# A gated mLSTM/S5 block: two operands transposed by VectorE alone, without the path through DRAM

## The chip, the cores and the metric

The kernel runs on one core of a Trainium2 chip. The metric is the device time of one execution in microseconds. Before the change the median of three runs is 1259.12 us (1258.21 to 1259.77).

## The reference, cut to what matters

One layer on a sequence of 256 rows with 2048 columns. The mLSTM and the S5 branch end in two projections to 2048 columns, which are gated and added (`merged`), projected by `w_out` and added to the residual; a SwiGLU feed-forward part with 5632 hidden columns follows.

```python
y_m = mlstm_branch(...) @ w_up_m          # 1024 -> 2048
y_s = s5_branch(...) @ w_up_s             # 512 -> 2048
g = sigmoid(p[..., c2:].reshape(b, s, 2, D) + b_gate)
merged = g[..., 0, :] * y_m + g[..., 1, :] * y_s
x = x + merged @ w_out                    # 2048 -> 2048
h2 = rms_norm(x, norm_ffn_g)
x = x + (silu(h2 @ w_ffn_gate) * (h2 @ w_ffn_up)) @ w_ffn_down
return rms_norm(x, norm_final_g)
```

## The kernel before

All weights come as blocks of 128 partitions x 1024 float32 columns (512 KB, two K tiles of 512 output columns), 432 of them in the order of use: `w_in`, the head matrices, `w_glu`, `w_up_s`, `w_up_m` (16 blocks), `w_out` (32), gate and up (176), down (88). A block is loaded by SyncE's queue (`emit_dma`, L144) into `raw`, which has three buffers; `emit_split` (L147) makes two reduced-precision parts of it, `hi` by a cast on ScalarE (L156) and `lo` = raw - hi on VectorE (recorded at L94, the line of the helper `TT`). Both have three buffers. `o2_block` (L160) then issues 12 matmuls for the block: two K tiles, two halves `tt` of 128 rows, and three products (activation hi x weight hi, hi x lo, lo x hi), at L100, into two accumulators of 128x512. A group of blocks with the same output columns is a chunk `n`: four blocks in `w_up_m`, eight in `w_out` and in the feed-forward matrices.

The activation is the stationary operand of a matmul, so it has to lie with its columns on the partitions. After a chunk of `w_up_m` the two tiles `merged` (rows x 512 columns, held in `gm`) have to be transposed to `mTh`/`mTl`, after a chunk of `w_out` the two tiles of the residual `x1` to `h2h`/`h2l`, and after each pair of gate and up chunks the hidden activation to `aT`.

`blocks_T` (L273) does that inside groups of 32 partitions: one VectorE instruction transposes all 32x32 blocks of a 128x512 tile in place of their group. The blocks must then change groups, and that goes through DRAM: `groups_dma` (L278) writes the tile out (`bounce`, L281) and reads four strided pieces back (L283), all on GpSimd's queue. `turn` (L969) is this path for `merged` and the hidden activation, `x1_T` (L1008) for the residual; a cast on ScalarE (L979, L1027) and a subtraction on VectorE then make the hi and lo parts. The steps are put off by `later`, which runs a step one or more weight blocks after it was handed in:

```python
def later(fn, delay=1):
    laters.append([delay, fn])
```

The program is built with a scheduler that orders the instructions of each engine by its own timeline. Within an engine they then run in that order, so a split of a weight block waits for whatever the scheduler put ahead of it on VectorE or ScalarE.

Of the kernel before, what the change touches and what calls it, by code (L numbers as in the profile page):

```python
# [13 lines left out]
AF = mybir.ActivationFunctionType  # L14
ALU = mybir.AluOpType
ADD, SUB, MUL, MAX, MIN = ALU.add, ALU.subtract, ALU.mult, ALU.max, ALU.min

P = 128
# [29 lines left out]
def block_kernel(ctx: ExitStack, tc: tile.TileContext, d, out):  # L48
    nc = tc.nc
    V, A, PE = nc.vector, nc.scalar, nc.tensor  # L50
# [12 lines left out]
    def nm(s):  # L63
        uid[0] += 1
        return f"{s}_{uid[0]}"

    def u8(shape, dt=F32, name="u"):
        return up.tile(shape, dt, tag="u8", name=nm(name), bufs=NU8)
# [10 lines left out]
    def m2(shape=(P, 512), dt=F32, name="m"):  # L79
        return tp.tile(list(shape), dt, tag="m2k", name=nm(name), bufs=NM2)  # L80

    def acc_tile():
        return pp.tile([P, 512], F32, tag="acc", name=nm("acc"), bufs=4)
# [4 lines left out]
    def TS(o, i, s1, s2=None, op0=MUL, op1=None):  # L88
        if op1 is None:
            return V.tensor_scalar(o, i, s1, None, op0=op0)  # L90
        return V.tensor_scalar(o, i, s1, s2, op0=op0, op1=op1)

    def TT(o, a, b, op):
        return V.tensor_tensor(o, a, b, op=op)  # L94

    def STT(o, a, s, b, op0, op1, **kw):
        return V.scalar_tensor_tensor(out=o, in0=a, scalar=s, in1=b, op0=op0, op1=op1, **kw)  # L97
# [4 lines left out]
    def f(ap):  # L102
        return ap.bitcast(F32)
# [5 lines left out]
    def pvs(n, i=None, w=1):  # L109
        a, b = PV[n]  # L110
        if i is None:
            return pv[:, a:b]
        return pv[:, a + i : a + i + w]
# [46 lines left out]
    def o2_block(acc, lhs, kts, hi, lo, first, last):  # L160
        n = len(kts)
        for q, kt in enumerate(kts):
            h = hi[:, q * 512 : (q + 1) * 512]
            l = lo[:, q * 512 : (q + 1) * 512]
            for tt in range(2):
                xh, xl = lhs(kt, tt)
                mm(acc[tt], xh, h, first and q == 0, False)
                mm(acc[tt], xh, l, False, False)
                mm(acc[tt], xl, h, False, last and q == n - 1)

    def lhs_of(hts, lts, per):
        def g(kt, tt):
            a, b = divmod(kt, per)
            s = slice(tt * 128, (tt + 1) * 128)
            return hts[a][:, b, s], lts[a][:, b, s]
        return g
# [64 lines left out]
    def rstd(o, ms, tag):  # L241
        w = ms.shape[-1]
        rc = cp.tile([P, w], F32, name=nm("rc"))
        V.reciprocal(rc, ms)
        A.activation(o, rc, AF.Sqrt)
        STT(rc, o, -0.5, ms, MUL, MUL)
        TT(rc, rc, o, MUL)
        STT(o, rc, 1.5, o, ADD, MUL)
# [24 lines left out]
    def blocks_T(o, i):  # L273
        V.transpose(o.rearrange("p j a c -> p a j c"), i.rearrange("p (a j c) -> p a j c", a=4, j=4))  # L274
# [3 lines left out]
    def groups_dma(dt_, st_):  # L278
        w = st_.shape[2]
        bounce = dp_.tile([P, 4, w], F32, tag=f"d{w}", name=nm("bounce"))  # L280
        nc.gpsimd.dma_start(bounce, st_)  # L281
        for j in range(4):
            nc.gpsimd.dma_start(  # L283
                dt_[32 * j : 32 * j + 32], bounce.rearrange("(i r) j x -> r i j x", i=4)[:, :, j]
            )
# [510 lines left out]
    cur = {}  # L796
# [47 lines left out]
    def gate_ap(key, tt, n):  # L844
        return cur[key][:, tt, n * 512 : n * 512 + 512]
# [105 lines left out]
    def upm_mm(i, nk, hi, lo):  # L951
        n, kp = nk
        if n == 0 and kp == 0:
            mlg.until("out")
            cur["mTh"] = [u8([P, 8, 256], F32R, name="mTh") for _ in range(2)]
            cur["mTl"] = [u8([P, 8, 256], F32R, name="mTl") for _ in range(2)]
        oh, ol = ml["out"]
        if kp == 0:
            cur["acc"] = [acc_tile(), acc_tile()]
        o2_block(cur["acc"], lhs_of([oh], [ol], 8), (2 * kp, 2 * kp + 1), hi, lo, kp == 0, kp == 3)  # L960
        if kp == 3:
            for tt in range(2):
                o = gate_ap("gm", tt, n)
                TT(o, cur["acc"][tt], o, MUL)
                TT(o, o, gate_ap("gs", tt, n), ADD)
                v = lambda a: a[n // 2][:, n % 2 * 4 : n % 2 * 4 + 4, :]
                turn(n, tt, o, v(cur["mTh"]), v(cur["mTl"]))

    def turn(n, tt, src, th, tl):  # L969
        st_ = m2([P, 4, 4, 32])  # L970
        blocks_T(st_, src)

        def move():
            dt_ = m2([P, 4, 4, 32])
            groups_dma(dt_.rearrange("p i a c -> p i (a c)"), st_.rearrange("p j a c -> p j (a c)"))

            def split():
                v = lambda a: a[:, :, tt * 128 : tt * 128 + 128].rearrange("p a (i c) -> p i a c", i=4)
                A.copy(v(th), dt_)  # L979
                TT(v(tl), dt_, f(v(th)), SUB)  # L980

            later(split)

        later(move)
# [3 lines left out]
    def out_mm(i, nk, hi, lo):  # L988
        n, kp = nk
        if n == 0 and kp == 0:  # L990
            cur["x1"] = u16([P, 2, 2048], name="x1")
            cur["h2h"] = [u8([P, 8, 256], F32R, name="h2h") for _ in range(2)]
            cur["h2l"] = [u8([P, 8, 256], F32R, name="h2l") for _ in range(2)]
        if kp == 0:
            cur["acc"] = [acc_tile(), acc_tile()]
            cs = slice(n * 512, n * 512 + 512)
            with tc.issue_after(wdma[0]):
                nc.sync.dma_start(cur["x1"][:, :, cs], d["x"].rearrange("(a p) c -> p a c", p=P)[:, :, cs])
        o2_block(cur["acc"], lhs_of(cur["mTh"], cur["mTl"], 8), (2 * kp, 2 * kp + 1), hi, lo, kp == 0, kp == 7)
        if kp == 7:  # L1000
            for tt in range(2):
                o = cur["x1"][:, tt, n * 512 : n * 512 + 512]
                TT(o, cur["acc"][tt], o, ADD)
                jk = t2()
                A.activation(jk, o, AF.Square, accum_out=ss2[:, tt, n : n + 1])
            later(lambda: x1_T(n))

    def x1_T(n):  # L1008
        sd = u8([P, 2, 1024], name="x1sd")
        st_ = sd[:, 0].rearrange("p (t j a c) -> p t j a c", j=4, t=2, a=4)  # L1010
        for tt in range(2):
            blocks_T(st_[:, tt], cur["x1"][:, tt, n * 512 : n * 512 + 512])

        def move():
            for tt in range(2):
                groups_dma(
                    sd[:, 1].rearrange("p (t i x) -> p t i x", t=2, i=4)[:, tt],
                    sd[:, 0].rearrange("p (t j x) -> p t j x", j=4, t=2)[:, tt],
                )
            later(split)  # L1020

        def split():
            d_ = sd[:, 1].rearrange("p (t i a c) -> p a (t i) c", i=4, t=2, a=4)
            for a in range(4):
                ct = 4 * n + a
                v = lambda h: h[ct // 8][:, ct % 8, :].rearrange("p (i c) -> p i c", c=32)
                A.activation(v(cur["h2h"]), d_[:, a], AF.Copy, scale=pvs("g2", ct))  # L1027
                STT(v(cur["h2l"]), d_[:, a], pvs("g2", ct), f(v(cur["h2h"])), MUL, SUB)

        later(move, 0)  # L1030
        if n == 3:
            s = cp.tile([P, 2], F32, name="ssum2")
            V.tensor_reduce(s, ss2, mybir.AxisListType.X, ADD)
            TS(s, s, 1.0 / D, EPS, MUL, ADD)
            rstd(r2, s, "r2")
# [117 lines left out]
    for b in range(2):  # L1153
        blocks.insert(len(blocks) - GLU, (d["w_glu"][0, b], glu_mm, (0, b)))
    add_mat("w_up_s", 4, 2, ups_mm)
    add_mat("w_up_m", 4, 4, upm_mm)
    add_mat("w_out", 4, 8, out_mm)
    fg, fu = ffn_mm("fg"), ffn_mm("fu")
# [10 lines left out]
    def later(fn, delay=1):  # L1169
        laters.append([delay, fn])  # L1170
# [63 lines left out]
    for i in range(len(blocks)):  # L1234
# [30 lines left out]
        for l in run:  # L1265
            l[1]()
        fn, (n, kp) = blocks[i][1], blocks[i][2]
        t = 2.59 if fn in (win_mm, ups_mm, upm_mm) else 1.31
        if fn is win_mm and kp == 7 and n > 4:
            t -= 1.3  # L1270
        if i < 6:
            t = 1.14 + SLACK + EB
# [82 lines left out]
```

## Time and profile before

| | |
|---|---|
| median of three runs | 1259.12 us |
| profiled execution | 1258.85 us, span 1257.1 us |
| TensorE busy | 1233.7 us (98%), 5738 matmuls |
| VectorE busy | 803.8 us (64%) |
| ScalarE busy | 604.0 us (48%) |
| GpSimd busy | 106.6 us (8%) |
| queue q1 (SyncE's loads) | 237.25 MB, 58.1% of 16 DMA engines |
| queue q0 (GpSimd's transfers) | 19.94 MB, 4.8% |

PE is TensorE, PEld its weight load, DVE is VectorE, ACT is ScalarE, POOL is GpSimd, SP is SyncE; a q behind the name is the engine's sequencer. The profile comes from one execution; a busy time is the sum over instructions without their overlap. TensorE's busy share says little by itself: its matmuls are pipelined, and a matmul lasts about 0.39 us while the next starts 0.23 us after it. Where a row merges several instructions (x2), its length runs from the start of the first to the end of the last.

### The profile page before, as it was taken

How to read it: one execution, taken by the hardware profiler on the slowest of the kernel's cores; microseconds unless marked ns; L12 is line 12 of the kernel's file. 1: busy time of each engine (PE TensorE's matmuls, PEld its weight loads, DVE VectorE, ACT ScalarE, POOL GpSimd, SP SyncE). 2: the span in 40 equal slices, each digit the busy share in tenths (PEclk: the TensorE clock that was granted, in tenths of full speed). 3: DMA queues.
4: the chain of work that ended last, by engine and by line, in shares of the span. 5: the costliest groups of instructions: out<-in, count | busy, mean ns of one | idle time of the engine just before them, and what ended most of it. 6: DMA issues, size and time to landing. Idle time of an engine off the chain costs nothing.

```text
span 1257.1 us, 15683 instructions
## 1 busy us (share of the span) xinstructions
PE 1233.7 (98%) x5738; PEld 1015.3 (81%) x5738; DVE 803.8 (64%) x1162; ACT 604.0 (48%) x752; POOL 106.6 (8%) x199
## 2 busy tenths in 40 slices
PE   7999999999999999989999999999999999999997
PEld 7777888887788878868888888888888888888885
DVE  8779945999877856645556555555555554554544
ACT  7574554446654445444344444434444443444433
POOL 0000000000000522211101100110111010000000
PEclk9999999999999999989999999999999999999999
DMA  7645655554555977877667766555765686666443
GB/s 265 208 137 178 194 184 182 167 160 143 190 182 193 280 265 256 286 239 224 217 203 228 222 212 217 187 184 204 245 228 183 225 279 198 196 198 199 152 161 141
DMA packets 75597, 258.19 MB, mean 205 GB/s; under 512 B 10496, under 2 KB 11264, under 8 KB 75520
## 3 DMA queue, kind: packets, MB, share of 16 engines
q1 hardware_dynamic: 67616, 237.25, 58.1%
q0 software_dynamic: 7904, 19.94, 4.8%
q8 instruction: 45, 0.74, 0.2%
q14 instruction: 32, 0.26, 0.1%
HBM read 245.09 MB, written 12.06 MB: 205 GB/s over the span
## 4 chain that ended last, share of the span: by engine, by line
PE 85%; DVE 6%; DMA 5%; issue 2%; ACT 1%; ACTq 0%; SPq 0%; DVEq 0%
PE acc L100 80%; PE aux L100 4%; DMA raw<-in_w_out_dram 4%; DVE lo L94 3%; ACT hi L156 1%; DMA raw<-in_w_ffn_gate_dram 1%; DVE xcT L97 1%; DVE stm L94 0%; DVE bu L94 0%; DMA raw<-in_w_up_m_dram 0%; DVE x L94 0%; DVE gm L94 0%; DMA raw<-in_w_in_dram 0%; PE aux L774 0%; DVE h2l L97 0%
## 5 line engine op out<-in xcount | busy, mean ns | idle before, releaser
L94 DVE TENSOR_TENSOR lo<-raw,hi 128x1024 fp32r<-128x1024 f32 x427 | 521.0, 1221 | 403.6 <-ACT hi L156 403.0
L156 ACT CAST hi<-raw 128x1024 fp32r<-128x1024 f32 x427 | 449.1, 1053 | 577.5 <-PE acc L100 488.9
L100 PE MATMUL acc<-lo,h2h 128*128 128x512 f32 x704 | 275.2, 391 | 0.6 <-DVE lo L94 0.5
L100 PE MATMUL acc<-hi,h2l 128*128 128x512 f32 x704 | 274.2, 390 | 0.0
L100 PE MATMUL acc<-hi,h2h 128*128 128x512 f32 x704 | 246.8, 391 | 4.2 <-ACT hi L156 4.2
L100 PE MATMUL acc<-hi,aT 128*128 128x512 f32 x664 | 204.6, 389 | 0.0
L100 PEld LDWEIGHTS acc<-hi,h2h 128*128 128x128 f32 x704 | 132.5, 189 | 32.7 <-ACT hi L156 5.3
L100 PEld LDWEIGHTS acc<-lo,h2h 128*128 128x128 f32 x704 | 132.7, 189 | 29.6 <-DVE lo L94 2.1
L100 PE MATMUL acc<-lo,hTh 128*128 128x512 f32 x384 | 153.6, 400 | 1.3 <-DVE lo L94 1.2
L100 PEld LDWEIGHTS acc<-hi,h2l 128*128 128x128 f32 x704 | 132.8, 189 | 27.4
L100 PE MATMUL acc<-hi,hTl 128*128 128x512 f32 x384 | 150.4, 392 | 0.0
L100 PEld LDWEIGHTS acc<-hi,aT 128*128 128x128 f32 x664 | 124.7, 188 | 25.9
L100 PE MATMUL acc<-hi,hTh 128*128 128x512 f32 x384 | 139.4, 393 | 0.0
L100 PE MATMUL acc<-lo,aT 128*128 128x512 f32 x332 | 129.1, 389 | 0.0
L100 PEld LDWEIGHTS acc<-lo,hTh 128*128 128x128 f32 x384 | 72.1, 188 | 22.1 <-DVE lo L94 4.0
L100 PEld LDWEIGHTS acc<-hi,hTh 128*128 128x128 f32 x384 | 71.7, 188 | 16.7 <-issue 2.0
L100 PEld LDWEIGHTS acc<-hi,hTl 128*128 128x128 f32 x384 | 72.2, 188 | 14.6 <-issue 0.7
L281 POOL DMA_DIRECT2D bounce<-m x30 | 16.9, 565 | 690.5 <-DVE m L274 690.2
L100 PEld LDWEIGHTS acc<-lo,aT 128*128 128x128 f32 x332 | 62.3, 188 | 12.9
L283 POOL DMA_DIRECT2D m<-bounce x120 | 65.6, 554 | 43.1 <-DMA bounce<-m 28.2
L100 PE MATMUL acc<-lo,mTh 128*128 128x512 f32 x128 | 50.0, 392 | 0.0
L100 PE MATMUL acc<-hi,mTl 128*128 128x512 f32 x128 | 49.5, 389 | 0.0
(246 smaller groups left out, 1077.7 us busy)
## 6 DMA issues: line engine op xcount, KB each, us to landing
raw<-in_w_in_dram SPq DMA_DIRECT2D x104, 512.0 KB, 3.5
raw<-in_w_ffn_gate_dram SPq DMA_DIRECT2D x88, 512.0 KB, 3.7
raw<-in_w_ffn_up_dram SPq DMA_DIRECT2D x88, 512.0 KB, 4.2
raw<-in_w_ffn_down_dram SPq DMA_DIRECT2D x88, 512.0 KB, 3.5
raw<-in_w_out_dram SPq DMA_DIRECT2D x32, 512.0 KB, 5.0
raw<-in_w_up_m_dram SPq DMA_DIRECT2D x16, 512.0 KB, 3.6
bounce<-m POOLq DMA_DIRECT2D x30, 256.0 KB, 4.1
m<-bounce POOLq DMA_DIRECT2D x120, 64.0 KB, 4.2
```

The lines of the kernel that those rows point to most:

```text
L94: return V.tensor_tensor(o, a, b, op=op)
L97: return V.scalar_tensor_tensor(out=o, in0=a, scalar=s, in1=b, op0=op0, op1=op1, **kw)
L100: return PE.matmul(o, l, r, start=start, stop=stop, skip_group_check=True)
L156: A.copy(hi, raw)
L281: nc.gpsimd.dma_start(bounce, st_)
L283: nc.gpsimd.dma_start(dt_[32 * j : 32 * j + 32], bounce.rearrange("(i r) j x -> r i j x", i=4)[:, :, j])
```

## The change

`merged` and the residual no longer go through DRAM. A new helper transposes a tile with 16 VectorE instructions. Each takes 32 partitions (group q) and four 32x32 blocks, every fourth one along the columns, and writes them transposed into another partition group j of the destination. After the sixteen the tile is fully transposed. `merged` gets a `turn_here` one block after its chunk, and in `x1_T` the first half is done at once and the second one block later; the products with the norm's gain are now made for each half (128 columns) instead of both (256). The hidden activation keeps `turn` and its path through DRAM.

```diff
-                turn(n, tt, o, v(cur["mTh"]), v(cur["mTl"]))
+                later(lambda tt=tt, o=o, th=v(cur["mTh"]), tl=v(cur["mTl"]): turn_here(n, tt, o, th, tl), tt)
+
+    def blocks_across(o, i):
+
+        v = i.rearrange("p (a j c) -> p a j c", a=4, j=4)
+        for q in range(4):
+            for j in range(4):
+                V.transpose(o[32 * j : 32 * j + 32, :, 32 * q : 32 * q + 32], v[32 * q : 32 * q + 32, :, j])
+
+    def turn_here(n, tt, src, th, tl):
+        dt_ = m2([P, 4, 128])
+        blocks_across(dt_, src)
+        v = lambda a: a[:, :, tt * 128 : tt * 128 + 128]
+        A.copy(v(th), dt_)
+        TT(v(tl), dt_, f(v(th)), SUB)
...
     def x1_T(n):
-        sd = u8([P, 2, 1024], name="x1sd")
...
-            for tt in range(2):
-                groups_dma(
...
+        d_ = u8([P, 4, 256], name="x1d")
+
+        def part(tt):
+            ts_ = slice(tt * 128, tt * 128 + 128)
+            blocks_across(d_[:, :, ts_], cur["x1"][:, tt, n * 512 : n * 512 + 512])
             for a in range(4):
                 ct = 4 * n + a
-                v = lambda h: h[ct // 8][:, ct % 8, :].rearrange("p (i c) -> p i c", c=32)
-                A.activation(v(cur["h2h"]), d_[:, a], AF.Copy, scale=pvs("g2", ct))
-                STT(v(cur["h2l"]), d_[:, a], pvs("g2", ct), f(v(cur["h2h"])), MUL, SUB)
-
-        later(move, 0)
+                v = lambda h: h[ct // 8][:, ct % 8, ts_]
+                A.activation(v(cur["h2h"]), d_[:, a, ts_], AF.Copy, scale=pvs("g2", ct))
+                STT(v(cur["h2l"]), d_[:, a, ts_], pvs("g2", ct), f(v(cur["h2h"])), MUL, SUB)
+
+        part(0)
+        later(lambda: part(1), 0)
```

On VectorE, at the seam between `w_up_m` and `w_out`, the last merged chunk stands like this before (`lo` is a weight split, `gm` the merged tile, `m` a transposed tile, `mTl` its low part):

```order
L94 TENSOR_TENSOR lo_3999<-raw_3922,hi_3998 128x1024
L94 TENSOR_TENSOR gm_2777<-acc_3928,gm_2777 128x512
L94 TENSOR_TENSOR gm_2777<-acc_3929,gm_2777 128x512
L94 TENSOR_TENSOR gm_2777<-gm_2777,gs_1153 128x512 x2
L94 TENSOR_TENSOR lo_4025<-raw_3956,hi_4024 128x1024
L274 STREAM_TRANSPOSE m_4016<-gm_2777 128x4x4x32
L274 STREAM_TRANSPOSE m_4020<-gm_2777 128x4x4x32
L94 TENSOR_TENSOR lo_4065<-raw_3974,hi_4064 128x1024
L94 TENSOR_TENSOR mTl_3645<-m_3942,mTh_3643 128x4x4x32
L94 TENSOR_TENSOR lo_4083<-raw_3996,hi_4082 128x1024
```

After the change the same engine has there:

```order
L94 TENSOR_TENSOR gm_2777<-acc_3975,gm_2777 128x512
L94 TENSOR_TENSOR gm_2777<-acc_3976,gm_2777 128x512
L94 TENSOR_TENSOR lo_4088<-raw_4008,hi_4087 128x1024
L94 TENSOR_TENSOR mTl_3645<-m_3989,mTh_3643 128x4x128
L94 TENSOR_TENSOR gm_2777<-gm_2777,gs_1153 128x512 x2
L974 STREAM_TRANSPOSE m_4066<-gm_2777 32x4x32 x16
L974 STREAM_TRANSPOSE m_4111<-gm_2777 32x4x32 x16
L94 TENSOR_TENSOR mTl_3645<-m_4066,mTh_3643 128x4x128
L94 TENSOR_TENSOR lo_4133<-raw_4026,hi_4132 128x1024
L94 TENSOR_TENSOR lo_4151<-raw_4044,hi_4150 128x1024
```

Two instructions between splits have become 32, and two additions and two low parts stand in the same gap.

On VectorE, after the first chunk of `w_out` (`x` is the residual, `x1sd` and `x1d` its transposed tiles, `h2l` the low part of the scaled activation), before:

```order
L94 TENSOR_TENSOR x_654_4028<-acc_4033,x_654_4028 128x512
L274 STREAM_TRANSPOSE x1sd_4219<-x_654_4028 128x4x4x32
L94 TENSOR_TENSOR lo_4201<-raw_4138,hi_4200 128x1024
L94 TENSOR_TENSOR lo_4225<-raw_4156,hi_4224 128x1024
L94 TENSOR_TENSOR x_654_4028<-acc_4034,x_654_4028 128x512
L94 TENSOR_TENSOR lo_4255<-raw_4174,hi_4254 128x1024
L274 STREAM_TRANSPOSE x1sd_4219<-x_654_4028 128x4x4x32
L94 TENSOR_TENSOR lo_4273<-raw_4198,hi_4272 128x1024
```

and after:

```order
L94 TENSOR_TENSOR x_641_4091<-acc_4096,x_641_4091 128x512
L94 TENSOR_TENSOR x_641_4091<-acc_4097,x_641_4091 128x512
L974 STREAM_TRANSPOSE x1d_4283<-x_641_4091 32x4x32 x10
L94 TENSOR_TENSOR lo_4265<-raw_4202,hi_4264 128x1024
L974 STREAM_TRANSPOSE x1d_4283<-x_641_4091 32x4x32 x12
L94 TENSOR_TENSOR lo_4311<-raw_4220,hi_4310 128x1024
L974 STREAM_TRANSPOSE x1d_4283<-x_641_4091 32x4x32 x10
L94 TENSOR_TENSOR lo_4353<-raw_4238,hi_4352 128x1024
L97 SCALAR_TENSOR_TENSOR h2l_4094<-x1d_4283,pv,h2h_4092 128x128 x4
L94 TENSOR_TENSOR lo_4371<-raw_4262,hi_4370 128x1024
L97 SCALAR_TENSOR_TENSOR h2l_4094<-x1d_4283,pv,h2h_4092 128x128 x4
L94 TENSOR_TENSOR lo_4389<-raw_4308,hi_4388 128x1024
```

The 32 transposes of a chunk are spread over three gaps between splits, and the products follow within the same chunk; before, they followed at the next chunk's eviction.

## Rows read from the trace of the kernel before

**Rows 1.** Stretches: us; busy us PE, PEld, DVE, ACT, POOL (instructions); clock, DMA, GB/s

```profile
400.00:440.00 40.00, 40.00 (x179) 33.10 (x178) 33.37 (x42) 17.56 (x20) 17.71 (x32) 1.00 0.87 268
440.00:546.00 106.00, 100.23 (x422) 79.63 (x420) 59.95 (x74) 51.28 (x72) 26.33 (x48) 0.97 0.81 275
546.00:1247.00 701.00, 700.48 (x3091) 580.17 (x3091) 381.10 (x373) 303.59 (x322) 60.44 (x110) 1.00 0.63 205
```

**Rows 2.** ScalarE's weight casts: group of 399.1 to 562.7 us, then timeline (start, length)

```profile
L156 ACT CAST hi<-raw 128x1024 fp32r<-128x1024 f32 x56 | 58.5, 1050 | 74.7 <-DMA raw<-in_w_out_dram 32.1 <-PE acc L100 25.0 <-DMA raw<-in_w_ffn_gate_dram 11.2
...
399.15 1.06 ACT L156 CAST hi<-raw 128x1024 fp32r<-128x1024 f32 x1 [1.67 <-PE acc L100]
...
560.07 1.05 ACT L156 CAST hi<-raw 128x1024 fp32r<-128x1024 f32 x1 [1.66 <-PE acc L100]
562.79 1.05 ACT L156 CAST hi<-raw 128x1024 fp32r<-128x1024 f32 x1 [1.67 <-PE acc L100]
```

**Rows 3.** Timeline of TensorE's matmuls at the start of the feed-forward part

```profile
534.83 0.39 PE L100 MATMUL acc<-hi,h2l 128*128 128x512 f32 x1
538.28 1.22 PE L100 MATMUL acc<-hi,h2h 128*128 128x512 f32 x2 [3.07 <-ACT hi L156]
...
543.55 0.63 PE L100 MATMUL acc<-hi,h2l 128*128 128x512 f32 x1
545.31 0.74 PE L100 MATMUL acc<-hi,h2h 128*128 128x512 f32 x2 [1.13 <-ACT hi L156]
```

**Rows 4.** The stretch behind TensorE's stop, columns as in rows 1

```profile
538.20:542.00 3.80, 3.68 (x8) 2.50 (x9) 3.59 (x3) 2.02 (x3) 1.95 (x4) 0.50 0.71 225
```

**Rows 5.** DMA queues and issues from 400 to 546 us (us to landing last)

```profile
q0 software_dynamic: 3328, 8.39, 17.6%
...
raw<-in_w_out_dram SPq DMA_DIRECT2D x32, 512.0 KB, 5.0
```

**Rows 6.** The same from 546 to 1000 us

```profile
q0 software_dynamic: 4160, 10.49, 7.0%
...
raw<-in_w_ffn_gate_dram SPq DMA_DIRECT2D x78, 512.0 KB, 3.6
```

**Rows 7.** Timeline of SyncE's loads at the start of the feed-forward part

```profile
525.03 4.83 SPq L144 DMA_DIRECT2D raw<-in_w_ffn_gate_dram  x4
```

**Rows 8.** Timeline of VectorE around merged chunks

```profile
398.66 1.28 DVE L94 TENSOR_TENSOR gm<-acc,gm 128x512 f32<-128x512 f32 x2
...
401.06 1.22 DVE L94 TENSOR_TENSOR lo<-raw,hi 128x1024 fp32r<-128x1024 f32 x1
402.19 1.29 DVE L274 STREAM_TRANSPOSE m<-gm 128x512 f32<-128x512 f32 x2
403.41 1.18 DVE L94 TENSOR_TENSOR lo<-raw,hi 128x1024 fp32r<-128x1024 f32 x1
...
419.09 0.68 DVE L94 TENSOR_TENSOR mTl<-m,mTh 128x512 fp32r<-128x512 f32 x1
419.69 1.22 DVE L94 TENSOR_TENSOR lo<-raw,hi 128x1024 fp32r<-128x1024 f32 x1
```

**Rows 9.** Timeline of VectorE where two halves of 64 partitions are written

```profile
42.29 0.85 DVE L94 TENSOR_TENSOR s5sp<-m,m 64x256 f32<-64x256 f32 x2
43.17 1.23 DVE L94 TENSOR_TENSOR lo<-raw,hi 128x1024 fp32r<-128x1024 f32 x1
44.31 0.75 DVE L94 TENSOR_TENSOR m<-s5c,s5sm 128x256 f32<-128x256 f32 x2
```

**Rows 10.** Timeline of VectorE, short operations of full height

```profile
286.72 0.28 DVE L97 SCALAR_TENSOR_TENSOR m<-aux,m 128x128 f32<-128x128 f32 x1
...
286.93 0.42 DVE L97 SCALAR_TENSOR_TENSOR m<-aux,m 128x256 f32<-128x256 f32 x1
```

**Rows 11.** Timeline of VectorE, products with the norm's gain

```profile
478.91 0.88 DVE L97 SCALAR_TENSOR_TENSOR h2l<-x1sd,pv,h2h 128x256 fp32r<-128x256 f32 x2
479.70 0.68 DVE L94 TENSOR_TENSOR x<-acc,x 128x512 f32<-128x512 f32 x1
```

More of the change, by code (lines that the diff above doesn't have):

```diff
@@ L1008, in x1_T @@
     def x1_T(n):
-        sd = u8([P, 2, 1024], name="x1sd")
-        st_ = sd[:, 0].rearrange("p (t j a c) -> p t j a c", j=4, t=2, a=4)
-        for tt in range(2):
-            blocks_T(st_[:, tt], cur["x1"][:, tt, n * 512 : n * 512 + 512])
-        def move():
-            for tt in range(2):
-                groups_dma(
[L1017 to L1023, printed above, removed]
+        d_ = u8([P, 4, 256], name="x1d")
+        def part(tt):
+            ts_ = slice(tt * 128, tt * 128 + 128)
+            blocks_across(d_[:, :, ts_], cur["x1"][:, tt, n * 512 : n * 512 + 512])
             for a in range(4):
                 ct = 4 * n + a
-                v = lambda h: h[ct // 8][:, ct % 8, :].rearrange("p (i c) -> p i c", c=32)
-                A.activation(v(cur["h2h"]), d_[:, a], AF.Copy, scale=pvs("g2", ct))
-                STT(v(cur["h2l"]), d_[:, a], pvs("g2", ct), f(v(cur["h2h"])), MUL, SUB)
-        later(move, 0)
+                v = lambda h: h[ct // 8][:, ct % 8, ts_]
[3 more added lines that the diff above has]
+        later(lambda: part(1), 0)
         if n == 3:
```

## The prediction

> **What bounds the kernel now.** I read the table by stretch first, then the pace of the weight blocks, then TensorE's gaps, then the DMA queues. TensorE is the bound almost everywhere: from 546 us on it is busy 700.48 of 701 us, and between 400 and 440 us all the time, while VectorE already runs 33.37 of 40 us there [rows 1]. The one place that loses time is the stretch from the first merged chunk to the start of the feed-forward part. ScalarE's weight split is its clock: a cast for block b+2 starts as a block ends, so its starts count blocks. From 399.15 to 562.79 us there are 56 intervals; the undisturbed interval is 562.79 - 560.07 = 2.72 us; 56 x 2.72 = 152.3, the stretch took 163.6, so 11.3 us are lost there [rows 2]. About 8 of them lie in one place: TensorE stops for 3.07 us before 538.28, then issues the twelve matmuls of a block from 538.28 to 543.98 (5.7 us instead of 2.72), then waits 1.13 us again [rows 3]. The slow block ran at a granted clock of 0.50, the 1.2 GHz level, right behind the stop [rows 4]. What it waited for is weights: in this stretch the path through DRAM (queue q0) takes 17.6% of the DMA engines' time and a weight block of w_out lands in 5.0 us [rows 5]; later q0 takes 7.0% and a block lands in 3.6 us [rows 6].
>
> **What the change removes.** Sixteen transposes of 128x512 (eight merged, eight residual tiles), and for each tile one write to DRAM and four reads back, with their waits. The 22 tiles of the feed-forward part keep that path. I credit the whole 11.3 us as given back, since without the DRAM path the load falls to that of the later stretch. Not all of it need come: SyncE also issues four weight blocks in 4.83 us at 525.03 [rows 7], and prefetches at that place stay in the new order. If they alone stop TensorE, the 8 us above stay (below).
>
> **What it adds: the price of one transpose.** Each tile becomes 16 VectorE instructions of 32 partitions x 128 columns: 256 in all. None like it stands in the trace, so I bound it.
> Ordinary neighbours overlap: a 128x512 operation at 419.09 is followed after 0.60, a 1024 one (401.06 to 402.19) after 1.13 us [rows 8]. That is 0.53 us per 512 columns, 0.13 us for 128, and 0.07 fixed: 0.21 with both, as the 128x128 operation at 286.72 shows, which lasts 0.28 and is followed after 0.21 [rows 10]. But where the output moves to another group of partitions the overlap is gone: the two 64x256 halves at 42.29 (first partitions 0 to 63, then 64 to 127) last 0.42 each, together take 0.85, and the full-height operation behind them starts at 43.17, 0.03 after their end, where the pair of 128x256 at 44.31 needs 0.75 [rows 9]. The new loop changes its output group at every instruction. So a transpose costs its own duration, 0.28, plus 0.03: 0.31 us. Ends: 0.13 (columns alone) and 0.43 (a held instruction of twice the columns); I take 0.31, the row that shares both the width and the moving output group.
>
> By the Trainium skill, page "VectorE: DVE Perf Modes", section "Two Vector instructions with no wait between them", a Vector instruction whose output starts in another 32-partition quadrant than the last one is held until all earlier ones have finished. The trace agrees at 42.29 us (0.85 against 0.75). It speaks against this change: with it the sum below is +35 us, with overlapping transposes +9.
>
> **The sum.** A chunk needs 32 transposes, 32 x 0.31 = 9.9 us.
> (a) Projection of the mLSTM branch, four weight blocks a chunk, 10.88 us of TensorE. VectorE needs four splits (4 x 1.13), four merge operations (2.40 from 398.66 to 401.06), two low parts of the merged tile (2 x 0.60): 8.1 us without transposes [rows 8], which fit before beside two transposes of 0.61. Now 18.0 us, 7.2 too many. That holds for the three intervals between the four merged chunks: 21.5 us. The splits' lead hides some of it: cast 1.05 and split 1.22 are done 2.3 us after a block's end and wanted 5.44 after it, so 3.1 us. Exposed: 18.4 us.
> (b) The seam to w_out. In the new order the low part of one tile, two additions, the 32 transposes of the last chunk and another low part all stand between two splits: 0.6 + 1.2 + 9.9 + 0.6 + 1.2 for the second split itself = 13.5 us. The lead is used up by (a), so TensorE has one block, 2.72 us: 10.8 exposed.
> (c) Each w_out chunk, eight blocks, 21.8 us. Two evictions (1.2), then ten, twelve and ten transposes with a split (1.13) behind each, then two groups of four products of 128 columns (0.26 each: 0.39 for 256 columns, two in 0.79 from 478.91 to 479.70 [rows 11], less 0.13). Against 2.72 a block the first three steps are over by 2.71, 2.13 and 1.51: 6.35, less the lead of 3.1, so 3.3 rounded up; the rest of the chunk catches up. Three chunks: 9.9. The fourth has the chain of seven small operations for the second norm among its transposes, 1 us more: 4.3.
> (d) A stop of the length of (b) brings the low clock: one block at 5.7 instead of 2.72, as above [rows 3, 4]: 3.0. The stops in (a) I price at nothing: there TensorE waits for VectorE, and a slower block only fills the next stop; if one is not covered, it is 3 us.
> ScalarE's side (32 products of 128 columns instead of 16 of 256, casts that now wait for transposes) I cost at nothing beside ScalarE's idle time, 22 of 40 us [rows 1]; its queue holds the next weight cast behind them, and that is VectorE's lateness, counted already. GpSimd only loses work.
> Total 18.4 + 10.8 + 9.9 + 4.3 + 3.0 = 46.4, less 11.3: +35.1. The profiled execution took 1258.85 us (span 1257.1 and 1.75 around it), 0.27 below the median of the three runs, 1259.12. Forecast 1258.85 + 35.1 = 1294 us.
>
> **Rivals.**
> 1. The transposes overlap, 0.21 each. (a) becomes 14.8 - 10.9 = 4.0, three times 11.9, less 3.1: 8.8; (b) 10.3 - 2.7 = 7.6; (c) 3.15 - 3.1, nearly nothing, three times 0.2 in all; the last chunk 1.0; (d) 3.0. 20.6 - 11.3 = +9.3: 1268 us. For it: all same-group neighbours overlap [rows 8, 10]. Against it: rows 9.
> 2. Faster: a transpose costs its columns alone, 0.13, and the stops stay short enough for the full clock. (a) 12.3 - 10.9, three times, less 3.1: 1.1; (b) 5.1; (c) nothing; 1.0 for the last chunk: 7.2 against 11.3 given back, 1255 us. The turning point is 0.16 us a transpose (1.28 us for each 0.01). For it: VectorE idles 52.7 of the 146 us from 400 to 546 [rows 1], enough for 256 x 0.2. Against it: the fixed part that every short row shows.
> 3. The stop at the feed-forward start was the prefetches', not the DRAM path's: 8 of the 11.3 stay, 1302 us. For it: rows 7. Against it: with TensorE later by 40 us the weights have had more time, and q0 is gone from the place.
> 4. The low clock is not hidden in (a): three stops there at 3 us each, 1303 us. For it: after the stop of 3.07 the clock fell at once. Against it: (a) is set by VectorE.
>
> **Chances.** The forecast with its own range of 1284 to 1304: 66 in 100. Rival 1: 15. Rival 2: 7. Rival 3: 5. Rival 4: 7. The range 1264 to 1305 takes in rival 1, the forecast, and most of 3 and 4; it leaves out rival 2 and what lies above 1305 (towards 0.43 us a transpose the sum would pass 1320), together under 2 in 10. Faster by over 0.2% (about what a measurement of this kernel can tell from no change): 0.06, most of rival 2; within 0.2%: 0.03, between rivals 1 and 2; slower: 0.91.
>
> **What would show it.** Right: 256 transposes of about 0.29 us, each starting where the last one ended; VectorE at 95% or more from the first merged chunk to the second w_out chunk; TensorE's idle time there put down to the split's low part on VectorE, no longer to weights; the longest stop, near 10 us, early in the first w_out chunk, with a granted clock of 0.5 behind it; weight blocks landing in under 4 us. From the feed-forward part's second chunk on, the 2.72 us pace unchanged. Wrong: transposes that start 0.2 us apart (rival 1); a stop at the first feed-forward blocks with ScalarE waiting for weights (rival 3); TensorE busy through the whole stretch (rival 2).

## The result, and the profile after

The changed kernel takes 1299.74 us (median of 6 runs, 1298.23 to 1301.68) against 1259.44 for the kernel before in the same session, a ratio of 1.032 with a 95% interval of 1.0307 to 1.0333. It is slower by 40 us; the forecast was +35 us, 1294 us. The profiled execution took 1300.99 us, 42.1 more than the profiled one of before.

The table by stretch, as [rows 1] (columns as there); the last stretch starts later because everything does:

```profile
400.00:440.00 40.00, 29.08 (x111) 22.55 (x110) 38.38 (x88) 11.98 (x14) 0.00 (x0) 0.87 0.35 118
440.00:546.00 106.00, 88.72 (x354) 70.30 (x353) 89.45 (x203) 41.75 (x62) 0.00 (x0) 0.92 0.48 156
...
590.00:1288.00 698.00, 698.00 (x3081) 577.98 (x3080) 379.36 (x369) 302.86 (x319) 60.42 (x110) 1.00 0.62 205
```

Between 400 and 440 us TensorE falls from 40.00 busy us to 29.08 while VectorE rises from 33.37 to 38.38 and GpSimd falls to nothing. From 590 us on TensorE is busy throughout, as before: all the loss lies ahead of it.

ScalarE's weight casts over the same blocks as in [rows 2], first the group from 399.2 to 605 us, then the first and the last in the timeline:

```profile
L156 ACT CAST hi<-raw 128x1024 fp32r<-128x1024 f32 x57 | 59.8, 1050 | 90.1 <-PE acc L100 60.6 <-DMA raw<-in_w_out_dram 16.7 <-DMA raw<-in_w_up_m_dram 4.8
```

```profile
399.38 1.06 ACT L156 CAST hi<-raw 128x1024 fp32r<-128x1024 f32 x1 [1.67 <-PE acc L100]
...
604.49 1.05 ACT L156 CAST hi<-raw 128x1024 fp32r<-128x1024 f32 x1 [1.67 <-PE acc L100]
```

57 casts are 56 intervals: 604.49 - 399.38 = 205.1 us, less 56 x 2.72 = 152.3, leaves 52.8 us lost, where 11.3 were lost before. The difference of 41.5 is the whole change but for 0.6 us. Where TensorE waited in it, from the waits between 395 and 620 us (total, times, longest):

```profile
PE acc L100 <- DVE lo L94: 36.0, 13, 6.2
PE acc L100 <- ACT hi L156: 0.7, 1, 0.7
```

TensorE now waits for VectorE's split; the wait for a weight to land and be cast, which made the stop in [rows 3], is down to 0.7 us. The remaining 16.1 of the 52.8 us lie behind the stops, mostly in matmuls at a lower clock (below). VectorE in the same stretch, first its groups, then its timeline at the first merged chunk, at the seam to `w_out`, and in the second chunk of `w_out`:

```profile
L974 DVE STREAM_TRANSPOSE x1d<-x 32x128 f32<-32x128 f32 x128 | 38.7, 303 | 1.9
L974 DVE STREAM_TRANSPOSE m<-gm 32x128 f32<-32x128 f32 x128 | 38.7, 303 | 1.7
```

```profile
398.89 1.28 DVE L94 TENSOR_TENSOR gm<-acc,gm 128x512 f32<-128x512 f32 x2
400.09 1.28 DVE L94 TENSOR_TENSOR gm<-gm,gs 128x512 f32<-128x512 f32 x2
401.30 1.22 DVE L94 TENSOR_TENSOR lo<-raw,hi 128x1024 fp32r<-128x1024 f32 x1
402.43 10.13 DVE L974 STREAM_TRANSPOSE m<-gm 32x128 f32<-32x128 f32 x32
412.59 0.69 DVE L94 TENSOR_TENSOR mTl<-m,mTh 128x512 fp32r<-128x512 f32 x1
413.20 3.49 DVE L94 TENSOR_TENSOR lo<-raw,hi 128x1024 fp32r<-128x1024 f32 x3
...
455.61 1.22 DVE L94 TENSOR_TENSOR lo<-raw,hi 128x1024 fp32r<-128x1024 f32 x1
456.74 0.69 DVE L94 TENSOR_TENSOR mTl<-m,mTh 128x512 fp32r<-128x512 f32 x1
457.34 1.29 DVE L94 TENSOR_TENSOR gm<-gm,gs 128x512 f32<-128x512 f32 x2
458.55 10.13 DVE L974 STREAM_TRANSPOSE m<-gm 32x128 f32<-32x128 f32 x32
468.70 0.69 DVE L94 TENSOR_TENSOR mTl<-m,mTh 128x512 fp32r<-128x512 f32 x1
469.31 3.49 DVE L94 TENSOR_TENSOR lo<-raw,hi 128x1024 fp32r<-128x1024 f32 x3
...
490.41 1.22 DVE L94 TENSOR_TENSOR lo<-raw,hi 128x1024 fp32r<-128x1024 f32 x1
491.66 3.80 DVE L974 STREAM_TRANSPOSE x1d<-x 32x128 f32<-32x128 f32 x12
495.50 1.23 DVE L94 TENSOR_TENSOR lo<-raw,hi 128x1024 fp32r<-128x1024 f32 x1
496.75 3.16 DVE L974 STREAM_TRANSPOSE x1d<-x 32x128 f32<-32x128 f32 x10
499.95 1.23 DVE L94 TENSOR_TENSOR lo<-raw,hi 128x1024 fp32r<-128x1024 f32 x1
```

32 transposes take 10.13 us: 303 ns each and 0.317 from start to start, so none overlaps the next. One chunk's transposes cost VectorE nearly what all four of its weight blocks take on TensorE (10.88 us). Between the splits at 455.61 and 469.31 stand 13.70 us.

TensorE's stops in the timeline, and the stretches behind some of them (columns as in [rows 1]):

```profile
414.47 0.80 PE L100 MATMUL acc<-lo,oh 128*128 128x512 f32 x1 [6.06 <-DVE lo L94]
...
434.95 0.80 PE L100 MATMUL acc<-lo,oh 128*128 128x512 f32 x1 [2.75 <-DVE lo L94]
...
453.41 0.80 PE L100 MATMUL acc<-lo,mTh 128*128 128x512 f32 x1 [5.74 <-DVE lo L94]
...
470.58 0.80 PE L100 MATMUL acc<-lo,mTh 128*128 128x512 f32 x1 [6.18 <-DVE lo L94]
...
523.13 0.50 PE L100 MATMUL acc<-lo,mTh 128*128 128x512 f32 x1 [2.08 <-DVE lo L94]
...
575.19 0.50 PE L100 MATMUL acc<-lo,h2h 128*128 128x512 f32 x1 [1.97 <-DVE lo L94]
...
581.22 0.50 PE L100 MATMUL acc<-lo,h2h 128*128 128x512 f32 x1 [3.02 <-DVE lo L94]
```

```profile
413.00:418.00 5.00, 3.53 (x9) 2.81 (x10) 4.42 (x6) 0.21 (x1) 0.00 (x0) 0.52 0.46 138
435.00:438.30 3.30, 3.30 (x8) 2.63 (x9) 3.30 (x5) 0.24 (x1) 0.00 (x0) 0.50 0.63 196
453.00:458.00 5.00, 4.59 (x11) 3.67 (x12) 5.00 (x8) 0.00 (x0) 0.00 (x0) 0.50 0.61 188
470.00:476.00 6.00, 5.42 (x13) 4.27 (x14) 3.40 (x4) 0.70 (x1) 0.00 (x0) 0.51 0.60 199
496.00:505.00 9.00, 6.81 (x29) 5.29 (x30) 8.81 (x22) 2.72 (x7) 0.00 (x0) 1.00 0.39 127
523.50:527.00 3.50, 3.50 (x10) 2.75 (x9) 3.36 (x10) 0.70 (x3) 0.00 (x0) 0.52 0.40 150
575.00:581.00 6.00, 3.01 (x12) 2.17 (x12) 5.75 (x18) 2.11 (x5) 0.00 (x0) 1.00 0.51 182
581.00:586.00 5.00, 4.78 (x14) 3.81 (x15) 3.78 (x10) 3.09 (x5) 0.00 (x0) 0.66 0.64 200
```

Behind the three stops of about 6 us the granted clock is 0.50 to 0.52, the 1.2 GHz level, as in [rows 4]; it is 0.50 and 0.52 behind the stops of 2.75 and 2.08 us as well, and behind the stop of 3.02 us 0.66 over the stretch. In the stretch with the stop of 1.97 us it stays at 1.00, as in the one with the two stops of 1.67 and 1.41 us (496 to 505). In the six stretches with a low clock, TensorE's busy time multiplied by the missing share of the clock gives an estimate of 12 us lost: most of the 16.1 above. The other 4 are not divided up here.

### The profile page after: what moved, and what is told of

The parts are those of the page before. It is cut to its first block, busy times and chain, and to the rows that moved or that the text cites. A ratio compares the mean times of both kernels' runs of the same rounds, so it can differ in the third digit from the quotient of the medians.

```text
span 1298.8 us, 15773 instructions
## 1 busy us (share of the span) xinstructions
PE 1244.5 (96%) x5738; PEld 1021.0 (79%) x5738; DVE 873.4 (67%) x1418; ACT 608.0 (47%) x768; POOL 62.5 (5%) x119
## 4 chain that ended last, share of the span: by engine, by line
PE 83%; DVE 12%; issue 2%; DMA 1%; ACT 1%; SPq 0%; ACTq 0%; DVEq 0%
PE acc L100 78%; PE aux L100 4%; DVE lo L94 3%; DVE m L974 3%; DVE x1d L974 3%; DMA raw<-in_w_out_dram 1%; DVE h2l L97 1%; ACT hi L156 1%; DVE gm L94 1%; DMA xt<-in_xT_dram 0%; DVE xcT L97 0%; DVE x L94 0%; DVE bu L94 0%; DMA raw<-in_w_ffn_gate_dram 0%; DVE stm L94 0%
## 5 line engine op out<-in xcount | busy, mean ns | idle before, releaser
L100 PE MATMUL acc<-lo,mTh 128*128 128x512 f32 x128 | 53.8, 421 | 20.7 <-DVE lo L94 20.7
L281 POOL DMA_DIRECT2D bounce<-m x22 | 12.4, 565 | 867.7 <-DVE m L274 867.7
L100 PE MATMUL acc<-hi,mTl 128*128 128x512 f32 x128 | 52.6, 411 | 0.0
L100 PEld LDWEIGHTS acc<-lo,mTh 128*128 128x128 f32 x128 | 25.7, 200 | 30.1 <-DVE lo L94 24.8
```

The source lines that it names most:

```text
L100: return PE.matmul(o, l, r, start=start, stop=stop, skip_group_check=True)
```

## The experiments

The theory: the price of the change is VectorE's time, 0.31 us a transpose, because a transpose whose group of partitions differs from the last one's does not overlap it. The rivals: it is a price of the instruction whatever its partitions; it is the number of columns; or the loss is made by transfers and prefetches.

**e1, transposes that stay in their group for four in a row.** The blocks don't change groups here.

```diff
-        for q in range(4):
-            for j in range(4):
-                V.transpose(o[32 * j : 32 * j + 32, :, 32 * q : 32 * q + 32], v[32 * q : 32 * q + 32, :, j])
+        for j in range(4):
+            for q in range(4):
+                V.transpose(o[32 * j : 32 * j + 32, :, 32 * q : 32 * q + 32], v[32 * j : 32 * j + 32, :, q])
```

> The same 256 transposes of 32x128, but each reads and writes the same group of partitions, and the group changes only at every fourth; the move to the other groups is left out, so the two operands are not the reference's. Theory (a transpose is held because its group of partitions moves): three of four start about 0.21 us apart, the fourth 0.32, mean 0.24; the steps of the sum worked again with 0.24 give 27 us lost instead of 46, so about 1276 us (1270 to 1283). Rival (it is the number of short transposes, whatever their group): 0.32 us apart as in the changed kernel, 1300 us.

Measured: 1276.06 us (1272.55 to 1276.45), ratio 1.0124 [1.0088, 1.0159]. VectorE's timeline at the first merged chunk, and the groups:

```profile
403.02 7.18 DVE L974 STREAM_TRANSPOSE m<-gm 32x128 f32<-32x128 f32 x32
```

```profile
L974 DVE STREAM_TRANSPOSE x1d<-x 32x128 f32<-32x128 f32 x128 | 29.3, 274 | 0.7
L974 DVE STREAM_TRANSPOSE m<-gm 32x128 f32<-32x128 f32 x128 | 28.4, 271 | 0.5
```

The same number of instructions of the same size start 0.222 us apart in the place of 0.317, less than the 0.271 that one lasts: they overlap. With that, 24 us of the 40 are gone, so the hold (a transpose waits for the one before to end) is the larger part of the loss. The recorded duration itself falls, from 303 to 271 and 274 ns in the mean.

**e2, the two loops exchanged.** The full computation; the output group now stays for four transposes, the input group moves each time.

```diff
-        for q in range(4):
-            for j in range(4):
+        for j in range(4):
+            for q in range(4):
```

> The changed kernel with the two loops exchanged: the output group stays for four transposes, the input group moves at every one. If only a moving output holds an instruction: mean 0.24 us, about 1276 us as with the moves left out. If a moving input holds it as well: 0.32 us apart throughout, 1300 us (1297 to 1303).

Measured: 1301.97 us (1299.62 to 1302.34), ratio 1.0324 [1.0293, 1.0356]. The first merged chunk on VectorE:

```profile
402.20 10.12 DVE L974 STREAM_TRANSPOSE m<-gm 32x128 f32<-32x128 f32 x32
```

A moving input holds as much as a moving output, of which alone the prediction spoke. In [rows 9] the kernel reads both inputs of a half from the same 64 partitions that it writes, so inputs and output move together there, and those rows could not tell them apart. By the Trainium skill, page "VectorE: DVE Perf Modes", section "Two Vector instructions with no wait between them", a first partition in another quadrant at an input or the output is enough; e2 agrees, 0.316 us apart. So neither order of these two loops helps.

**e3, no move at all.** One 128x512 transpose of blocks in place for each tile, as before, and neither the path through DRAM nor the short transposes. The move between groups is left out.

```diff
-        blocks_across(dt_, src)
+        blocks_T(dt_, src)
...
-            blocks_across(d_[:, :, ts_], cur["x1"][:, tt, n * 512 : n * 512 + 512])
+            blocks_T(d_[:, tt], cur["x1"][:, tt, n * 512 : n * 512 + 512])
```

> Each tile is transposed in its own groups by one instruction of 128x512, as before, and neither DRAM nor the 16 short transposes follow: the move between groups is left out, so the two operands are not the reference's. It shows what the path through DRAM cost by itself. Theory: all 11.3 us come back, 1248 us (1246 to 1250), and the weight splits keep the 2.72 us pace through the whole stretch. Rival (the stop at the start of the feed-forward part is the prefetches'): about 8 us stay there, 1256 us.

Measured: 1248.61 us (1248.13 to 1249.01), ratio 0.9905 [0.9876, 0.9934]: 10.9 us below the 1259.49 of before in that session. The table by stretch:

```profile
400.00:440.00 40.00, 40.00 (x178) 33.14 (x177) 35.36 (x46) 19.98 (x23) 0.00 (x0) 1.00 0.61 203
440.00:560.00 120.00, 120.00 (x531) 99.41 (x530) 73.15 (x100) 63.91 (x98) 0.00 (x0) 1.00 0.68 235
```

TensorE has no wait from 400 to 560 us, with every weight load and prefetch of the changed kernel still in place. The path through DRAM did cost what [rows 2] showed, and rival 3 (the prefetches make the stop) is false.

**e4, the same transposes by TensorE.** The full computation; four 128x128 transposes against the identity for each tile, into PSUM, and the hi and lo parts read from there.

```diff
-        blocks_across(dt_, src)
+        ps_ = aux()
+        for a in range(4):
+            PE.transpose(ps_[:, a * 128 : a * 128 + 128], src[:, a * 128 : a * 128 + 128], ident)
...
```

The residual's tiles are changed in the same way.

> Both operands are transposed by TensorE, four 128x128 a tile into PSUM, 64 in all; the cast and the subtraction read PSUM. No short transposes and no path through DRAM. The trace of before has eight TensorE transposes in 0.87 us, 0.11 each: 7.0 us on TensorE. Theory: the stretch is free of other stops, 1248 + 7 = 1255 us (1252 to 1258), a little faster than before. Rival: TensorE waits for the merged tile in front of its transposes, some 0.5 us for each of 16 tiles, 1263 us.

Measured: 1255.84 us (1255.38 to 1256.07), ratio 0.9967 [0.9953, 0.9981]. The transposes in the groups of TensorE:

```profile
L1031 PE MATMUL aux<-cst,x 128*128 128x128 f32 x32 | 4.8, 272 | 0.0
L979 PE MATMUL aux<-cst,gm 128*128 128x128 f32 x32 | 4.1, 272 | 0.0
```

No wait of TensorE is left between 395 and 620 us. Against e3 the 64 transposes cost 1255.84 - 1248.61 = 7.2 us, 0.113 each, on the engine that is the bound, and this beats both kernels: sixteen short ones on VectorE (16 x 0.317 = 5.1 us a tile) stand against four here (0.45 us).

**e5 and e6, one half of the change each.** In e5 the residual keeps the path of before, in e6 `merged` does.

```diff
# e5, in x1_T, against the changed kernel
-            blocks_across(d_[:, :, ts_], cur["x1"][:, tt, n * 512 : n * 512 + 512])
+            blocks_T(st_[:, tt], cur["x1"][:, tt, n * 512 : n * 512 + 512])
...
+                groups_dma(
...
# e6, against the changed kernel
-                later(lambda tt=tt, o=o, th=v(cur["mTh"]), tl=v(cur["mTl"]): turn_here(n, tt, o, th, tl), tt)
+                turn(n, tt, o, v(cur["mTh"]), v(cur["mTl"]))
```

> The merged branch alone goes by the 16 short transposes; the residual keeps its way through DRAM. My theory (VectorE's time is the price, 0.317 us a transpose): the merged part and the seam lose 32.8 us against the weight casts, of which before lost some 3.3, and the residual's part loses what it lost before, some 8: about 1259.4 - 3.3 + 32.8 = 1289 us. Rival (the residual's way through DRAM costs TensorE its stop only since the transfers meet other loads there, and they now start later): 1281. If most of the loss sits in the residual's part, it would be under 1275.

> The residual alone goes by the 16 short transposes; the merged branch keeps its way through DRAM. My theory: the four chunks of the last projection lose the 20 us that the trace of after shows there, and the 8 us of the residual's way through DRAM are gone: about 1259.4 - 8 + 20 = 1271 us; by the 14.2 us of the prediction for this part it would be 1266. Together with the merged branch alone it should make up the whole change of +40.

Measured: e5 1289.86 us (1289.65 to 1290.78), ratio 1.0241 [1.0215, 1.0266]; e6 1269.95 us (1268.58 to 1270.44), ratio 1.0081 [1.006, 1.0103]. The stretches of e5, then of e6:

```profile
400.00:440.00 40.00, 30.34 (x108) 23.33 (x107) 38.39 (x88) 11.36 (x14) 0.00 (x0) 0.84 0.37 118
440.00:490.00 50.00, 38.28 (x149) 30.58 (x148) 40.88 (x89) 16.67 (x21) 1.25 (x2) 0.85 0.44 141
490.00:546.00 56.00, 56.00 (x249) 46.37 (x248) 31.99 (x36) 26.80 (x37) 15.30 (x28) 1.00 0.86 269
```

```profile
400.00:440.00 40.00, 40.00 (x178) 33.10 (x178) 34.34 (x44) 18.64 (x20) 17.67 (x32) 1.00 0.85 269
440.00:490.00 50.00, 45.29 (x196) 36.15 (x195) 38.42 (x80) 23.90 (x37) 4.37 (x8) 1.00 0.60 202
490.00:546.00 56.00, 50.20 (x203) 39.25 (x202) 48.96 (x112) 25.06 (x43) 0.00 (x0) 0.94 0.67 218
```

Each loses time where its own transposes are: e5 has TensorE busy for all of 490 to 546 us, e6 for all of 400 to 440. Between 440 and 490 us both lose, e5 at the seam, and e6, which reaches `w_out` sooner, with the transposes of its first chunk. Against 1259.11 they are +30.8 and +10.8, together +41.6, the whole change of +40.3 within the spread of the runs. The rival of 1281 for e5 is out: the residual's way through DRAM still costs TensorE its stop at the feed-forward start, as the waits of e5 between 395 and 640 us show (total, times, longest):

```profile
PE acc L100 <- ACT hi L156: 5.1, 3, 3.3
```

**e7, both row halves in one transpose.** 16 transposes of 32 partitions x 256 columns for a chunk. Both row halves of a chunk are then turned in one step, so the second half is turned earlier than in the changed kernel.

```diff
-                V.transpose(o[32 * j : 32 * j + 32, :, 32 * q : 32 * q + 32], v[32 * q : 32 * q + 32, :, j])
+                V.transpose(w[32 * j : 32 * j + 32, :, :, 32 * q : 32 * q + 32], v[32 * q : 32 * q + 32, :, :, j])
...
```

> The whole change, with both halves of the rows in one instruction: 16 transposes of 32 partitions x 256 columns in a chunk in the place of 32 of 32 x 128. If the hold and a length by columns make the price (0.303 with 45 ns more for 128 columns more and some 15 ns between them, taken with the longer element walk as 0.45 us each, 7.2 us a chunk in the place of 10.1): 1248.6 + 10 + 8 + 3 + 6 = about 1276 us, 1268 to 1282. Rival, the price is one of the instruction whatever its columns (0.32 us, 5.1 us a chunk): about 1262. Rival, by columns alone: no gain, 1300.

Measured: 1276.81 us (1273.81 to 1277.1), ratio 1.0132 [1.0108, 1.0156]. VectorE's timeline and group:

```profile
402.78 7.18 DVE L976 STREAM_TRANSPOSE md<-gm 32x256 f32<-32x256 f32 x16
```

```profile
L976 DVE STREAM_TRANSPOSE md<-gm 32x256 f32<-32x256 f32 x64 | 27.9, 436 | 0.8
```

0.449 us each: 128 columns more cost 0.132 us, the columns' own time in [rows 8], and the rest of 0.317 is a fixed 0.185 for a held instruction. The 45 ns of the expectation stand in no row; its 0.45 us in all came out. The chunk of 7.18 us is as long as e1's, and so is the time of the kernel: whether half the instructions go or most of the holds, the loss follows VectorE's time.

## Why the prediction was right, and which terms were off

By its time alone the run would fit rivals 3 and 4 (1302 and 1303 us) better than the forecast of 1294. What bears the forecast out is the mechanism: e3 rules out rival 3, and VectorE's rows below rule out rival 4.

**The give-back, 11.3 us: right.** e3 gave 10.9.

**The price, 0.31 us a transpose, taken from [rows 9] over the 0.21 of [rows 10]: right.** It is 0.317, from 303 ns and 14 between. e1, at 0.222, shows that the moving group makes the difference.

**(a), (b) and (d), the merged part: right in sum, not in its split.** From the eviction of the first merged chunk (398.89) to that of the first `w_out` chunk (486.04) the changed kernel takes 87.15 us for 20 blocks (54.4): 32.75 lost, predicted 18.4 + 10.8 + 3.0 = 32.2. VectorE sets the pace of it, nearly without a pause up to the end of the gap at the seam:

```profile
398.90:473.40 74.50, 51.66 (x191) 40.26 (x191) 71.88 (x169) 21.48 (x24) 0.00 (x0) 0.86 0.34 114
```

Its busy time between the evictions of the four merged chunks is 17.95, 17.53 and 17.96 us (predicted 18.0), and the gap between splits at the seam is 13.70 us (predicted 13.5). But the loss divides in another way. Up to the fourth merged eviction (454.41) 55.5 us go for 12 blocks (32.6): 22.9 lost, where (a) had 18.4. From there to 486.04 it is 31.6 us for 8 blocks (21.8): 9.9 lost, where (b) and (d) had 13.8. The two misses cancel: VectorE's chain, whose length the sum had right, fixes the end of the last stop, and (a) and (b) only share out what TensorE did meanwhile. The stop "near 10 us" isn't there: TensorE works on three blocks from 453.41 to 464.40 while VectorE is in the gap, where (b) gave it one, and the stop is 6.18 us at 470.58. The stop before it, 5.74 us at 453.41, comes from the third chunk's transposes and so belongs to (a). Three stops in (a) brought the low clock, as rival 4 had it (at 414.47, 434.95 and 453.41), but VectorE was idle for only 2.6 us of the 74.5, so they can't have cost rival 4's 9 us: a slower block filled the next stop. The low clock behind 470.58 is the one spell of (d): 5.42 busy us at 0.51, an estimated 2.7 lost, predicted 3.0.

**(c), the `w_out` chunks: the mechanism right, the size too small.** Predicted 9.9 + 4.3 = 14.2; measured 78.5 us from 486.04 to 564.55 for three chunks (65.3), 13.2 lost, and 6.9 in the last, which is what is left of the 52.8: 20.1. These 5.9 us are the shortfall of the forecast. Two things were missing. A split between transposes gets no overlap either, since the transpose behind it starts in another group: from 490.41 to 491.66 are 1.25 us, not 1.13, and from split to split 5.09 and 4.45 us where the sum had 4.85 and 4.23. With the first step that is some 0.6 us a chunk, about 2.5 in all. And the stops were priced at the full clock: in the fourth chunk a stop of 3.02 us is followed by 0.66, an estimated 1.6 us. The second chunk has a low clock too, behind its stop of 2.08 us, but it lost 4.4 us (512.40 to 538.55), no more than the first and the third (4.6 and 4.2), so there the clock cost nothing that shows. Some 1.8 of the 5.9 us stay open. e6 alone lost 18.8 by the same count (1269.95 - 1259.11, with the 8 of the prediction given back), against 14.2.

**The marks.** Right: the transposes end to end, the stops put down to `lo`, the pace after 590 us. Wrong: VectorE at 95% or more only up to 473.4 us, not to the second `w_out` chunk; the longest stop 6.18 us, though where it was expected and with the clock of 0.51 behind it; weight blocks of `w_out` landing in 4.1 us (before 5.0), not under 4.

Rivals 1 and 2 (0.21 and 0.13 us) asked for overlapping transposes; e1, where three in four do overlap, shows what that would have brought, and even there the kernel is slower than before.

## What to carry to other kernels

A block-wise transpose that moves data between groups of 32 partitions is priced not by its elements alone but by instructions that don't overlap (here 0.185 us for each, and 0.132 for each 128 columns): count them, take the duration and gap of a pair whose group moves, and compare the sum with the engine's slack between two instructions that the bound engine waits for, not with its idle share over the stage. Before moving work off a slow path, price it on every engine that could take it: here the busiest one, TensorE, was the cheapest place (7.2 us in all), since there a whole tile is four instructions.

## What the runs showed of the hardware that was not expected

A held transpose is recorded as longer, not only later: 303 ns with the group moving at every instruction, 271 to 274 in the mean where it moves at every fourth. And two kernels whose chunks cost VectorE the same 7.18 us, by half the instructions (e7) or by fewer holds (e1), came out within 0.8 us of each other, 1276.81 and 1276.06.
